# Modulation columns of four chunks by TensorE from the loaded weights, and x loaded first, in the head of a two-layer diffusion backbone

## The chip, the cores and the metric

The kernel runs on one core of one Trainium2 chip, as one program for both layers. The time is the device time of one execution in microseconds, taken as the median of several runs. The profile comes from one more execution, recorded by the hardware profiler. TensorE (PE in the profile, its weight loads PEld) multiplies matrices into PSUM, VectorE (DVE), ScalarE (ACT) and GpSimd (POOL) work element by element, and SyncE (SP) issues most of the transfers.

## The reference

Two layers work on 1024 latent tokens and 256 context tokens of width 1024. The head of the kernel computes the beginning of layer 0: shift and scale of the modulation, the normalised and modulated tokens, and the first quarter of the `v` half of `h @ w_in`.

```python
def rms_norm(x, g):
    xf = x.astype(jnp.float32)
    y = xf * lax.rsqrt(jnp.mean(xf * xf, axis=-1, keepdims=True) + EPS)
    return (y * g.astype(jnp.float32)).astype(x.dtype)

def modulate(h, shift, scale):
    return h * (1 + scale) + shift

def chunk_mlp(h, w_in, ln_g, ln_b, w_s, b_s, w_out):
    z = jax.nn.gelu(h @ w_in)
    u, v = jnp.split(z, 2, axis=-1)
    v = layer_norm(v, ln_g, ln_b)
    ...

    silu_c = jax.nn.silu(c)
    for i in range(DEPTH):
        mod_lat = (silu_c @ ada_w[i] + ada_b[i])[:, None, :]
        ...
        sh1, sc1, g1, sh2, sc2, g2 = jnp.split(mod_lat, 6, axis=-1)
        ...
        h = modulate(rms_norm(x, norm_g[i, 0]), sh1, sc1)
        ...
            y = chunk_mlp(h, a_w_in[j], a_ln_g[j], a_ln_b[j], a_w_s[j], a_b_s[j], a_w_out[j])
```

All is float32. The kernel splits each float32 operand of the large products into a high and a low part of type float32r and forms three products (high by high, high by low, low by high).

## The kernel before, in words

The ten token tiles of 128 rows are worked in two groups: five latent tiles (LAT), then three latent and two context tiles. The head (lines 580 to 780 of the kernel) is the part of the first group that the change touches. It works in eight chunks of 128 model columns (k = 0 to 7).

Names in the head:

- `xn0` holds the five token tiles, loaded by five transfers (lines 679 and 680) and normalised row by row: ACT squares and sums, GpSimd takes the power, DVE multiplies (lines 686 to 688).
- `flip_x(k)` transposes chunk k of the five tiles on TensorE (five transposes) into `pts[k]`, a PSUM tile of two banks. There are two such tiles, and one is taken by the head's sums, so `flip_x(k + 1)` waits until `x_hi(k)` has read `pts[k]`.
- `AdaBlock(k0, nk)` loads the columns of ada_w for shift and scale of `nk` chunks (two of 128 or 256 columns at a time), `accum` multiplies the eight row blocks by the conditioning vector and sums them on DVE, `total` sums over the partitions on TensorE with a vector of ones (`2 * nk` matmuls of one column), and `finish` adds bias and norm weight on DVE into the modulation columns. The buffers of the loaded columns have the tag `act`, six of them, 512 KB each.
- `x_hi(k)` applies scale and shift on ACT (two instructions) and casts the high part; `x_lo(k)` subtracts for the low part on DVE.
- `w_load(u)`, `w_hi(u)`, `w_lo(u)` load a block of 256 rows of w_in into one of three buffers `raw` and split it, on ACT and DVE; block u serves the chunks 2u and 2u + 1.
- `head_mm(k, part)` is one of three groups of five float32r matmuls with 512 columns, one per token tile, summed over all k in five banks.

The order of the work in the head is written by hand: `pins` holds the names of VectorE, ScalarE, TensorE and SyncE (line 584), and each of these engines then keeps the order of the program. A step that waits therefore holds up what stands behind it on its engine. Lines 676 to 778 are that order. Before, there are five blocks: b0 and b1 of one chunk, b2, b3 and b4 of two chunks each. Behind the head `pins` is cleared, and `gmlp` goes on with the same buffers `raw` for w_in and for the columns of the next modulations.

## Time and profile before

| | before |
|---|---|
| median of 3 runs | 2856.6 us (2850.05 to 2860.5) |
| profiled execution | 2860.88 us, span 2859.1 us |
| DVE SCALAR_TENSOR_TENSOR on the blocks' columns (`acc<-act`) | 35 in the head, 22.5 us |
| TensorE 128x1 matmuls in the head (`psA<-ones,acc`) | 32, 4.8 us |
| last matmul of the head starts | 65.07 us |
| mean granted clock | 0.988 |

In the page each engine has its busy time, its share of the span and its number of instructions. A row of a stretch gives the time and number of instructions of each engine in that stretch, then the clock granted to TensorE (1 is full), the share of the DMA engines and what they moved. A row of the timeline gives start, duration, engine, operation, tile written and tiles read, and in brackets the idle time ahead of it and what ended it. Nearly every instruction has line 50, that of a helper; the tile names tell them apart: `y` is `xn0`, `act` the loaded columns, `acc` the sums on DVE, `big` the high and low parts of x, `wh` and `wl` those of the weights.

### The profile page before, as it was taken

To read this page: it belongs to the slowest core of one execution; us is meant where nothing else is said; L and a number is where in the kernel's file an instruction comes from. 1 tells how busy PE (TensorE), PEld (TensorE's weight loads), DVE (VectorE), ACT (ScalarE), POOL (GpSimd) and SP (SyncE) were. 2 spreads that over 40 slices of the span, in tenths; PEclk is the share of its full clock that TensorE was granted. 3 is DMA by queue.
4 is the path that set the end of the run, shared out by engine and by line. 5 is a ranking of instruction groups with operands and counts; after the bars stand their busy time and mean duration, and the time that the engine had idled before them with its cause. 6 is when DMAs were issued, how large, how long until landed. Compare 5 with 4: busy or idle time off the path is not lost.

```text
span 2859.1 us, 40314 instructions
## 1 busy us (share of the span) xinstructions
PE 2741.8 (96%) x14570; PEld 2354.1 (82%) x14570; DVE 2221.8 (78%) x3466; ACT 1391.2 (49%) x2291; POOL 616.6 (22%) x806
## 2 busy tenths in 40 slices
PE   7999999999989999999999899999998999999998
PEld 5798887898889888888788778888887888888786
DVE  6567684787779899887776568898887788888776
ACT  4333242232367444455434545777876444445433
POOL 1164021360210212111000124543333121220000
PEclk9999999999999999999999999999999999999999
DMA  7775457554488355467855565347577345545753
GB/s 260 251 234 166 145 161 227 177 167 131 171 249 240 103 170 162 157 217 238 287 169 184 188 212 186 115 145 239 181 242 220 126 162 182 160 144 198 248 177 125
DMA packets 436335, 537.13 MB, mean 188 GB/s; under 512 B 20004, under 2 KB 300452, under 8 KB 436135
## 3 DMA queue, kind: packets, MB, share of 16 engines
q1 hardware_dynamic: 379575, 470.84, 51.4%
q10 hardware_dynamic: 55408, 59.52, 6.2%
q0 software_dynamic: 1152, 4.19, 0.4%
q8 instruction: 115, 1.88, 0.3%
q14 instruction: 85, 0.70, 0.1%
HBM read 414.40 MB, written 120.07 MB: 187 GB/s over the span
## 4 chain that ended last, share of the span: by engine, by line
PE 65%; DVE 13%; DMA 11%; ACT 5%; issue 4%; POOL 2%; SPq 1%; ACTq 0%; DVEq 0%; POOLq 0%
PE psB L50 48%; PE psA L50 16%; DVE row L50 3%; DVE wl L50 3%; DMA raw<-in_ada_w_dram 3%; DVE tmp L50 1%; DVE acc L50 1%; ACT wh L50 1%; ACT tmp L50 1%; DMA xT<-row 1%; DMA raw<-in_a_w_in_dram 1%; DVE y L50 1%; POOL sm L50 1%; DMA raw<-in_f_w_up_dram 1%; DMA raw<-in_f_w_down_dram 1%
## 5 line engine op out<-in xcount | busy, mean ns | idle before, releaser
L50 PE MATMUL psB<-cmb,wh 128*128 128x512 f32 (+2 forms) x2584 | 750.3, 374 | 7.2 <-ACT row L50 6.2
L50 PEld LDWEIGHTS psB<-cmb,wh 128*128 128x128 f32 x2584 | 471.9, 188 | 98.4 <-ACT row L50 8.1
L50 PE MATMUL psB<-cmb,wl 128*128 128x512 f32 (+2 forms) x1292 | 483.2, 374 | 0.2 <-DVE wl L50 0.2
L50 ACT CAST wh<-raw 128x1024 fp32r<-128x1024 f32 (+1 forms) x313 | 265.1, 863 | 441.6 <-PE psB L50 165.5
L50 DVE TENSOR_TENSOR wl<-raw,wh 128x1024 fp32r<-128x1024 f32 (+1 forms) x313 | 307.6, 997 | 106.6 <-ACT wh L50 104.9
L50 PEld LDWEIGHTS psB<-cmb,wl 128*128 128x128 f32 x1292 | 243.2, 188 | 44.0 <-DVE wl L50 0.8
L50 PE MATMUL psB<-wh,big 128*128 128x512 f32 x816 | 271.1, 398 | 3.7 <-ACT big L50 1.3
L50 ACT CAST wh<-row 128x1024 fp32r<-128x1024 f32 (+1 forms) x196 | 162.5, 834 | 186.8 <-DVE row L50 92.3
L50 PE MATMUL psB<-wh,act 128*128 128x512 f32 x640 | 200.1, 390 | 0.8 <-DVE tmp L50 0.8
L50 DVE TENSOR_TENSOR wl<-row,wh 128x1024 fp32r<-128x1024 f32 (+1 forms) x196 | 185.2, 948 | 12.2 <-ACT wh L50 11.8
L50 PE MATMUL psA<-big,wh 128*128 128x320 f32 x1024 | 193.2, 310 | 0.3 <-ACT row L50 0.3
L50 POOL TENSOR_TENSOR row<-raw,raw 128x512 f32<-128x512 f32 x44 | 68.5, 1558 | 574.2 <-DMA raw<-in_f_w_up_dram 490.8
L50 PEld LDWEIGHTS psB<-wh,big 128*128 128x128 f32 x816 | 154.3, 190 | 39.9 <-ACT tmp L50 2.4
L50 DVE SCALAR_TENSOR_TENSOR acc<-raw,ccols,acc 128x1024 f32<-128x1024 f32 x98 | 126.7, 1311 | 75.8 <-DMA raw<-in_ada_w_dram 75.5
L50 DVE SCALAR_TENSOR_TENSOR row<-row,cwcols,row 128x1024 f32<-128x1024 f32 (+2 forms) x142 | 152.6, 1075 | 39.2 <-ACT row L50 22.7
L50 ACT CAST ah<-raw 128x1024 fp32r<-128x1024 f32 x80 | 77.6, 974 | 201.6 <-PE psB L50 80.8
L50 DVE TENSOR_TENSOR row<-row,row 128x512 f32<-128x512 f32 (+4 forms) x169 | 155.9, 926 | 19.9 <-DMA row<-actd 12.2
L50 POOL TENSOR_SCALAR row<-row,sm,sm 128x128 f32<-128x128 f32 x160 | 144.1, 919 | 115.2 <-DMA row<-vscr 99.3
L50 PEld LDWEIGHTS psA<-big,wh 128*128 128x128 f32 x1024 | 159.9, 188 | 0.7 <-ACT row L50 0.5
L50 PE MATMUL psB<-wl,big 128*128 128x512 f32 x408 | 157.2, 395 | 0.9 <-DVE wl L50 0.9
L50 DVE TENSOR_TENSOR al<-raw,ah 128x1024 fp32r<-128x1024 f32 x80 | 90.2, 1128 | 71.9 <-ACT ah L50 71.6
L50 PE MATMUL psB<-row,wh 128*128 128x256 f32 x744 | 136.9, 286 | 8.2 <-ACT wh L50 6.7
(279 smaller groups left out, 6226.0 us busy)
## 6 DMA issues: line engine op xcount, KB each, us to landing
raw<-in_f_w_up_dram SPq DMA_DIRECT2D x121, 512.0 KB, 4.8
raw<-in_ada_w_dram SPq DMA_DIRECT2D x88, 512.0 KB, 4.4
raw<-in_a_w_in_dram SPq DMA_DIRECT2D x64, 512.0 KB, 4.8
wh<-woscr SPq DMA_DIRECT2D x48, 512.0 KB, 4.1
row<-actd SPq DMA_DIRECT2D x44, 512.0 KB, 5.5
actc<-row SPq DMA_DIRECT2D x44, 512.0 KB, 4.1
raw<-actc SPq DMA_DIRECT2D x40, 512.0 KB, 3.6
actd<-row SPq DMA_DIRECT2D x39, 512.0 KB, 2.7
```

Source lines behind the costliest of these rows:

```text
L50: ins = fn(*a, **kw)
```

## The change

A new class `AdaColumn` loads shift and scale columns of one chunk (two transfers of 512 KB) and forms the modulation columns on TensorE alone: for each of the two, eight matmuls with the loaded 128x128 block of ada_w as the stationary operand and one column of the conditioning vector as the moving one, summed in PSUM. Chunks 0 to 3 are made this way (b0 to b3); chunks 4 and 5 (b4) and 6 and 7 (b6) stay with `AdaBlock`. The rows of x are loaded ahead of the first columns. `w_hi(0)` is cast in two halves and comes after `x_hi(0)`. The order of the head is written anew.

```diff
+    def finish_block(block):
+        k0, nk = block.k0, block.nk
+        p = pts[k0][:, 1, 256:256 + 2 * nk]
+        for s in (1, 0):
+            finish_cols(0, s, 0, p[:, s * nk:(s + 1) * nk], slice(k0, k0 + nk))
+
...
+    class AdaColumn:
+        def __init__(self, k0):
+            self.k0, self.nk, self.rv = k0, 1, {}
             for s in (1, 0):
-                finish_cols(0, s, 0, p[:, s * nk:(s + 1) * nk], slice(k0, k0 + nk))
+                self.rv[s] = t_act((P, KD, P), F32)
+                Q.dma_start(self.rv[s], ada_w[0, :, s * D + k0 * P:s * D + (k0 + 1) * P]
+                            .rearrange("(k p) n -> p k n", p=P))
+
+        def total(self):
+            p = pts[self.k0][:, 1, 256:258]
+            for s in (1, 0):
+                for k in range(KD):
+                    T.matmul(p[:, s:s + 1], self.rv[s][:, k, :], ccols[:, k:k + 1], start=(k == 0), stop=(k == KD - 1))
+
+        def finish(self):
+            finish_block(self)
...
-        S.copy(hi, raws[nb, u])
+        for c in ((0, 512), (512, 1024)) if (nb, u) == (0, 0) else ((0, 1024),):
+            S.copy(hi[:, slice(*c)], raws[nb, u][:, slice(*c)])
...
-    b0 = AdaBlock(0, 1)
     adab, aR = load_rows([ada_b.rearrange("l (k p) -> (l k) p", p=P)])
     ngr, nR = load_rows([norm_g.rearrange("l i (k p) -> (l i k) p", p=P)])
     for i, t in enumerate(LAT):
         Q.dma_start(xn0[:, i, :], src_row(0, t))
+    b0 = AdaColumn(0)
     w_load(0)
-    b1 = AdaBlock(1, 1)
+    b1 = AdaColumn(1)
+    b2 = AdaColumn(2)
...
```

The new order, from the first transposes to where it joins the old one:

```python
    flip_x(0); b0.total(); b0.finish(); x_hi(0); w_hi(0); x_lo(0); w_lo(0)
    b3 = AdaColumn(3); w_load(1)
    head_mm(0, 0); flip_x(1); b1.total(); b1.finish(); x_hi(1)
    head_mm(0, 1); head_mm(0, 2); x_lo(1)
    b4 = AdaBlock(4, 2)
    flip_x(2); b2.total(); b2.finish(); x_hi(2); w_hi(1); b4.accum(range(0, 2))
    head_mm(1, 0); head_mm(1, 1); head_mm(1, 2); x_lo(2); w_lo(1)
    w_load(2); b6 = AdaBlock(6, 2)
    flip_x(3); b3.total(); b3.finish(); x_hi(3); b4.accum(range(2, 4))
    head_mm(2, 0); head_mm(2, 1); head_mm(2, 2); x_lo(3); b4.accum(range(4, 8)); w_hi(2)
    flip_x(4); head_mm(3, 0); head_mm(3, 1); b4.total(); b4.finish(); x_hi(4); w_lo(2)
    head_mm(3, 2); x_lo(4); b6.accum(range(0, 2)); w_load(3)
    flip_x(5); x_hi(5); x_lo(5); b6.accum(range(2, 5))
    head_mm(4, 0); head_mm(4, 1); head_mm(4, 2)
    flip_x(6); w_hi(3); b6.accum(range(5, 8))
    head_mm(5, 0); b6.total(); b6.finish(); x_hi(6); w_lo(3); x_lo(6)
    head_mm(5, 1); head_mm(5, 2); w_load(0, 1); flip_x(7)
```

From `flip_x(7)` on the order is as before.

## The prediction

> **What bounds the kernel now.** I read the page first, then the head by stretches, then the chain of waits, then single instructions of TensorE in order of time.

> ```profile
> span 2859.1 us, 40314 instructions
> ...
> PE 2741.8 (96%) x14570; PEld 2354.1 (82%) x14570; DVE 2221.8 (78%) x3466; ACT 1391.2 (49%) x2291; POOL 616.6 (22%) x806
> ```

> ```profile
> core 0: us, PE busy (x) PEld busy (x) DVE busy (x) ACT busy (x) POOL busy (x), PEclk, DMA share, GB/s
> 31.90:65.10 33.20, 31.64 (x160) 24.99 (x159) 25.52 (x42) 16.39 (x24) 0.00 (x0) 1.00 0.66 214
> ```

> The whole is TensorE's: 96% busy. The change touches only the head, from the start to the last head matmul. TensorE is busy for 31.64 of the 33.20 us between 31.90 and 65.10; DVE, which the change relieves, has 7.7 us to spare there. Before 31.90 it is otherwise:

> ```profile
> 6.36 8.23 DMA y<-in_x_dram
> ...
> 24.01 2.57 DMA act<-in_ada_w_dram
> ```

> The chain runs through the loading of x, then through DVE's sums that wait for columns of ada_w. So the head has two parts: up to about 32 us it waits for data, from there TensorE is the bound. Work taken from DVE helps the first part, work given to TensorE lengthens the second. The same in single instructions:

> ```profile
> 19.44 0.47 PE L50 MATMUL psA<-ident,y 128*128 128x128 f32 x1 [0.99 <-DVE y L50]
> 19.71 0.85 PE L50 MATMUL psA<-ones,acc 128*128 128x1 f32 x4
> ...
> 23.08 2.08 PE L50 MATMUL psB<-wh,big 128*128 128x512 f32 x4 [1.34 <-ACT big L50]
> ...
> 26.73 1.02 PE L50 MATMUL psA<-ones,acc 128*128 128x1 f32 x4 [1.15 <-DVE acc L50]
> 27.61 2.05 PE L50 MATMUL psB<-wh,big 128*128 128x512 f32 x4
> ...
> 29.89 1.91 PE L50 MATMUL psB<-wl,big 128*128 128x512 f32 x4
> ...
> 31.94 0.71 PE L50 MATMUL psA<-ident,y 128*128 128x128 f32 x5
> ...
> 35.12 1.05 PE L50 MATMUL psA<-ones,acc 128*128 128x1 f32 x8 [0.15 <-DVE acc L50]
> 36.04 1.17 PE L50 MATMUL psB<-wl,big 128*128 128x512 f32 x4
> ...
> 39.93 1.09 PE L50 MATMUL psB<-wh,big 128*128 128x512 f32 x4
> ...
> 41.08 1.07 PE L50 MATMUL psB<-wl,big 128*128 128x512 f32 x4
> ...
> 42.22 0.71 PE L50 MATMUL psA<-ident,y 128*128 128x128 f32 x5
> 42.69 1.18 PE L50 MATMUL psB<-wh,big 128*128 128x512 f32 x4
> ```

> Two prices can be read off. A head group of five 512-column matmuls takes 41.08 - 39.93 = 1.15 us late in the head, but 31.94 - 29.89 = 2.05 to 29.89 - 27.61 = 2.28 us early: up to 31.8 us TensorE runs at half clock, though the granted-clock column has no record there. And `b0.total()`, two matmuls in the source, is four in the trace: an F32 matmul is issued twice. Each 128x1 pair (weight load and matmul) takes (27.61 - 26.73)/4 = 0.22 us at half clock and (36.04 - 35.12)/8 = 0.115 at full.

> **The change part by part.** First, the columns 0 to 3. DVE loses the sums of b0, b1 and b2:

> ```profile
> L50 DVE SCALAR_TENSOR_TENSOR acc<-act,ccols,acc 128x512 f32<-128x512 f32 x21 | 15.7, 748 | 0.4
> ...
> L50 DVE SCALAR_TENSOR_TENSOR acc<-act,ccols,acc 128x256 f32<-128x256 f32 x14 | 6.8, 484 | 0.5
> ```

> About 6.8 us of the small ones and a third of the large (5.2) go, with their starts some 13 us of DVE, none of it on the path after 32 us. TensorE gets, per column, 2 streams x 8 chunks = 16 F32 matmuls = 32 pairs: 7.0 us at half clock, 3.7 at full. Removed are 4, 4 and 8 pairs.

> Second, x first. The issues that go from ahead of x, and x's own:

> ```profile
> 1.52 2.05 SPq L50 DMA_DIRECT2D act<-in_ada_w_dram  x4
> ...
> 4.79 3.15 SPq L50 DMA_DIRECT2D y<-in_x_dram  x5
> ```

> ```profile
> 15.86 1.06 ACT L50 ACTIVATE tmp<-y 128x1024 bf16<-128x1024 f32 x1
> ```

> ```profile
> 15.00:20.00 5.00, 1.98 (x6) 1.11 (x7) 2.26 (x3) 2.96 (x5) 3.08 (x6) 1.00 1.09 343
> ```

> x is issued 2.1 us earlier, and 1.05 MB no longer lie ahead of it, 3.0 us at 343 GB/s. If the rows of x only share the engines with what is issued behind them, it is nothing; I take 2.5, near the 2.1 of the issue: the last transpose of chunk 0 ends at 17.4 instead of 19.9. b0's 1.05 MB now land 3 us behind the last row of x, which was squared at 15.86 and now at 13.4 or so: 16.4, just in time.

> Third, the way to the first matmul. `b0.total()` runs with nothing before it but transposes, at half clock: 17.4 + 32 x 0.22 = 24.4. From the end of that step (19.71 + 0.85) to the first head matmul it was 23.08 - 20.56 = 2.5 us (finish, modulation, cast). `w_hi(0)`, which ran before, now follows `x_hi(0)` on ACT, and its first half is waited for:

> ```profile
> 17.15 1.04 ACT L50 CAST wh<-raw 128x1024 fp32r<-128x1024 f32 x1
> ```

> Half of 1.04 is 0.5, so the first head matmul starts at 24.4 + 3.0 = 27.4 instead of 23.08.

> Fourth, from there to the end of the head, first all at full clock: 24 groups x 1.15 = 27.6; 7 transposing steps x 0.5 (42.69 - 42.22) = 3.5; b1 to b3, 96 x 0.115 = 11.0; b4 and b6 8 pairs each, 1.8. Waits: one of the 0.5 us kind remains (chunk 5 behind a block's chunk 4), and one is new.

> ```profile
> PE psA L50 <- ACT tmp L50: 1.4, 3, 0.5
> ```

> ```profile
> 45.08 0.95 PE L50 MATMUL psA<-ones,acc 128*128 128x1 f32 x8
> ```

> ```profile
> L50 DVE TENSOR_SCALAR acc<-act,ccols 128x512 f32<-128x512 f32 x3 | 1.4, 481 | 0.0
> ```

> ```profile
> 48.49 0.82 DVE L50 TENSOR_TENSOR big<-tmp,big 128x640 fp32r<-128x640 f32 x1 [0.56 <-ACT big L50]
> ```

> The new one: all eight sums of b6 stand behind `x_lo(4)` on DVE, and b6's total is one group earlier than its like was. The like of `x_lo(4)` ended at 49.31, 3.3 us after the block total of 45.08 that feeds it (ended 46.03); then come 0.48 + 7 x 0.75 = 5.7 us of sums and 0.82 of `x_lo(5)`: 9.8 us, while TensorE has five groups, two transposing steps and a wait, 7.2. It waits 2.6. Sum: 27.6 + 3.5 + 11.0 + 1.8 + 0.5 + 2.6 = 47.0, head end 74.4. It now ends here, with the last matmul's successor at 65.30:

> ```profile
> 65.07 0.39 PE L50 MATMUL psA<-wl,big 128*128 128x512 f32 x1
> 65.30 0.39 PE L50 MATMUL psA<-wh,big 128*128 128x512 f32 x1
> ```

> That is +9.1 with the clock left at full after the first column. But the clock does not stay:

> ```profile
> 35.24:38.66 3.42, 2.96 (x18) 2.17 (x18) 2.05 (x7) 1.86 (x3) 0.00 (x0) 1.00 0.88 291
> ...
> 96.68:100.10 3.42, 0.00 (x0) 0.00 (x0) 2.30 (x4) 0.00 (x0) 0.00 (x0) 1.00 0.89 320
> 100.10:103.51 3.41, 2.99 (x7) 2.41 (x8) 0.81 (x3) 0.00 (x0) 0.00 (x0) 0.50 0.44 142
> ...
> 127.40:130.82 3.42, 3.29 (x23) 2.93 (x23) 1.86 (x3) 1.42 (x3) 2.81 (x4) 1.00 0.44 136
> 130.82:134.23 3.41, 3.41 (x14) 2.91 (x13) 1.92 (x3) 0.38 (x2) 0.00 (x0) 0.50 1.07 326
> ```

> ```profile
> 127.67 1.95 PE L50 MATMUL psB<-ones,acc 128*128 128x1 f32 x16
> 129.48 0.48 PE L50 MATMUL psB<-wl,big 128*128 128x512 f32 x1
> ```

> The clock changes on a grid of 3.41 us. An idle stretch (96.68) is followed by one at 0.50, and that, with 2.99 us of wide matmuls in it, by full clock again. The stretch at 127.40 is what matters: TensorE was busy for 3.29 of 3.42 us, 1.8 of them with 16 one-column pairs and 1.3 (39%) with wide matmuls, and the next stretch is at 0.50 all the same. So such pairs count for next to nothing. At 35.24 five wide matmuls (1.15 us, 34%), five transposes and 8 pairs kept the clock: the border lies near 35 to 40% of wide work. In the changed kernel a column and its transposing step make 3.7 + 0.5 = 4.2 us without wide work, longer than a stretch; two stretches hold at most 6.8 - 4.2 = 2.6 us of it, so one of them falls below the border unless they split it evenly. [...]

> The price: from 27.4 on, `mm(0,0)`, b1 and `mm(0,1)`, `mm(0,2)` are at half clock, since no stretch full of wide work comes before the last two: 3 x 1.0 + 32 x 0.105 + 0.6 (two transposing steps, 0.3 each by estimate) = 7.0. Then b2 and b3 each bring one or two stretches at half, 1.7 to 3.4 us; I take 2.6 each. Together 12.2, head end 86.6, +21.3. With a lucky phase of the grid (up during `mm(0,1)`, one stretch per column or none) about 12; unlucky 23.

> Edits at nothing: eight issues of 512 KB replace 16 of 256 KB on SP. b3's buffers are b0's, so on SP `w_load(1)` and b4 stand behind b0's total (24.4); they are wanted after 45 us. b4's last buffers wait for b2's total, about 47, wanted near 60. If either came late, TensorE would wait for it one to one. DVE's b4 sums stand ahead of `x_lo(2)` and `w_lo(1)`, and their data wait for b1's total (37) and land about 42, ahead of b2's finish.

> Does the delay last to the end? The loads after the head go through three buffers, freed by `w_lo(3)` and `w_lo(0, 1)`, both of which stand behind head steps. I find nothing behind the head that starts by itself, so I carry the delay whole. The profiled execution took 2860.88 us, 1.8 beyond its span, and would come to 2882.2; it is 4.3 over the median of 2856.6. On the median the sum is 2877.9, taken as 2878, 0.7% slower.

> **The rivals.** (1) The pairs do count as work, and the clock stays. Then b0 lifts it itself after one stretch: 3.4 + 16.5 x 0.115 = 5.3 us, first head matmul at 25.7, head end at 25.7 + 47.0 = 72.7, +7.4: 2864, no measurable change. For it speaks the stretch at 35.24, against it that at 127.40.

> (2) Not slower: the pairs go nearly free, because weight loads slip in beside other work, and the head is freed of DVE's sums and of ada_w ahead of x. With a price p per pair the head ends at 17.4 + 32p + 3.0 + 36.0 + 96p = 56.4 + 128p. It decides at p = 0.07 us: below, the change gains, at most 8.9 us: 2848. The rows show 0.113 (16 pairs in 1.81 us) with wide matmuls on both sides. Even so it would hardly pass 0.5%.

> (3) The order of DVE or SP stalls TensorE more than I see (b4 or b6 late): +25 to +30, 2882 to 2887.

> **How the numbers follow.** The forecast 0.62, rival 1 0.24, rival 2 0.08, rival 3 0.06. About 0.5% (14.3 us) is what a measurement of this kernel can tell from no change. Slower by more: the forecast except its lucky end (0.57), rival 3 (0.06), a little of rival 1: 0.64. Faster by more: 0.04, a part of rival 2 with the 10 us by which runs differ. The rest is 0.32. The range runs from rival 1 less 4 us, 2860, to the unlucky phase and the scatter above it, 2884.

> **What would show it.** Right: 32 pairs per column in TensorE's timeline, 0.2 us each in column 0; first head matmul near 27, last near 85; granted clock of 0.5 behind columns 2 and 3; a wait of 2 to 3 us for DVE before b6's total; transposes of chunk 0 done near 17. Wrong: the granted clock at 1.00 from 30 us on (rival 1), pairs under 0.07 us (rival 2), a head that is late but a span that is not.

## The result and the profile after

| | before | after |
|---|---|---|
| median of 6 runs each | 2851.07 us (2846.16 to 2860.5) | 2875.44 us (2864.74 to 2879.28) |
| ratio | | 1.0078, 95% interval 1.0054 to 1.0102 |
| span of the profiled execution | 2859.1 us | 2872.3 us |
| last matmul of the head starts | 65.07 us | 83.92 us |

By the medians the change makes the kernel slower by 24 us (15 to 29 by the interval of the ratio); 2878 was forecast. The page of the changed kernel, its span and first row:

```profile
span 2872.3 us, 40499 instructions
...
PE 2757.4 (96%) x14682; PEld 2371.0 (83%) x14682; DVE 2208.6 (77%) x3445; ACT 1390.5 (48%) x2292; POOL 620.3 (22%) x806
```

TensorE has 112 more matmuls: 4 columns of 32 pairs are 128, and 16 went. It is 15.6 us busier. DVE is 13.2 us less busy, near the 13 us that were counted. The single instructions of TensorE in the head, in order of time:

```profile
16.39 0.48 PE L50 MATMUL psA<-ident,y 128*128 128x128 f32 x1 [0.99 <-DVE y L50]
16.66 6.83 PE L50 MATMUL psA<-ccols,act 128*128 128x1 f32 x32
26.52 2.08 PE L50 MATMUL psB<-wh,big 128*128 128x512 f32 x4 [3.03 <-ACT wh L50]
...
29.88 6.83 PE L50 MATMUL psA<-ccols,act 128*128 128x1 f32 x32
36.57 2.05 PE L50 MATMUL psB<-wh,big 128*128 128x512 f32 x4
...
38.85 1.91 PE L50 MATMUL psB<-wl,big 128*128 128x512 f32 x4
...
41.95 3.82 PE L50 MATMUL psA<-ccols,act 128*128 128x1 f32 x32
45.63 2.05 PE L50 MATMUL psB<-wh,big 128*128 128x512 f32 x4
...
51.11 3.63 PE L50 MATMUL psA<-ccols,act 128*128 128x1 f32 x32
54.60 1.32 PE L50 MATMUL psB<-wh,big 128*128 128x512 f32 x4
...
73.47 1.05 PE L50 MATMUL psA<-ones,acc 128*128 128x1 f32 x8 [2.02 <-DVE acc L50]
...
83.92 0.39 PE L50 MATMUL psA<-wl,big 128*128 128x512 f32 x1
```

The four columns are the four rows with x32: 6.8 us at half clock for columns 0 and 1, 3.8 and 3.6 at full for 2 and 3. A wide matmul is one of 512 columns, and a head group has five of them. The group at 36.57 takes 2.05 us for its first four, as does the one at 45.63, behind column 2: half clock. The row at 73.47 is the foreseen wait for DVE's eight sums of b6. In the traces before and after, the granted clock is recorded as 1.00 or 0.50 and nothing else, and each of the 22 records of a trace starts a whole number of 3.413 us behind the first one. Stretches of this grid, with the granted clock behind the POOL column:

```profile
38.41:41.83 3.42, 3.42 (x11) 2.72 (x10) 0.83 (x1) 0.72 (x1) 0.00 (x0) 1.00 0.38 126
41.83:45.24 3.41, 3.41 (x33) 3.41 (x32) 0.00 (x0) 0.00 (x0) 0.00 (x0) 1.00 0.08 19
45.24:48.65 3.41, 3.41 (x11) 2.83 (x11) 1.95 (x6) 2.31 (x4) 0.00 (x0) 0.50 0.88 286
48.65:52.07 3.42, 3.42 (x24) 2.98 (x23) 1.63 (x2) 0.50 (x1) 0.00 (x0) 1.00 0.45 156
52.07:55.48 3.41, 3.41 (x28) 3.27 (x29) 0.67 (x4) 0.19 (x1) 0.00 (x0) 1.00 0.40 120
55.48:58.90 3.42, 3.42 (x10) 2.64 (x9) 2.78 (x5) 2.62 (x4) 0.00 (x0) 0.50 0.84 271
```

In every row TensorE is busy throughout, and yet the clock falls to 0.50 behind the two stretches that hold columns 2 and 3. (At 38.41 the column shows 1.00 for want of a record, the first being at 41.83, as it is at 31.83 in the kernel before; the wide group of 38.85, 1.91 us for its first four, tells that it is half.) DVE meanwhile idles: 0.00 at 41.83.

### The profile page after: what moved, and what is told of

Its sections match the earlier page's. It is cut to its first block, busy times and chain, and to the rows that moved or that the text cites. A ratio compares the mean times of both kernels' runs of the same rounds, so it can differ in the third digit from the quotient of the medians.

```text
span 2872.3 us, 40499 instructions
## 1 busy us (share of the span) xinstructions
PE 2757.4 (96%) x14682; PEld 2371.0 (83%) x14682; DVE 2208.6 (77%) x3445; ACT 1390.5 (48%) x2292; POOL 620.3 (22%) x806
## 4 chain that ended last, share of the span: by engine, by line
PE 63%; DVE 13%; DMA 11%; issue 5%; ACT 4%; POOL 2%; SPq 0%; ACTq 0%; DVEq 0%; POOLq 0%
PE psB L50 46%; PE psA L50 17%; DVE row L50 4%; DMA raw<-in_ada_w_dram 4%; DVE wl L50 3%; DVE acc L50 1%; DMA raw<-in_a_w_in_dram 1%; ACT wh L50 1%; DVE tmp L50 1%; DMA xT<-row 1%; DMA raw<-in_f_w_up_dram 1%; ACT tmp L50 1%; POOL sm L50 1%; DVE y L50 1%; ACT row L50 1%
## 5 line engine op out<-in xcount | busy, mean ns | idle before, releaser
L50 PE MATMUL psB<-cmb,wh 128*128 128x512 f32 (+2 forms) x2584 | 749.3, 374 | 9.7 <-ACT row L50 7.5
L50 PEld LDWEIGHTS psB<-cmb,wh 128*128 128x128 f32 x2584 | 471.0, 188 | 101.3 <-ACT row L50 10.2
L50 PE MATMUL psB<-cmb,wl 128*128 128x512 f32 (+2 forms) x1292 | 482.5, 373 | 0.1
L50 ACT CAST wh<-raw 128x1024 fp32r<-128x1024 f32 (+1 forms) x314 | 265.3, 861 | 430.6 <-PE psB L50 171.4
L50 DVE TENSOR_TENSOR wl<-raw,wh 128x1024 fp32r<-128x1024 f32 (+1 forms) x313 | 307.8, 998 | 108.1 <-ACT wh L50 107.0
L50 PEld LDWEIGHTS psB<-cmb,wl 128*128 128x128 f32 x1292 | 242.9, 188 | 43.8 <-DVE wl L50 0.5
L50 PE MATMUL psB<-wh,big 128*128 128x512 f32 x816 | 273.0, 401 | 5.9 <-ACT wh L50 3.7
L50 ACT CAST wh<-row 128x1024 fp32r<-128x1024 f32 (+1 forms) x196 | 162.6, 835 | 188.9 <-DVE row L50 97.6
L50 PE MATMUL psB<-wh,act 128*128 128x512 f32 x640 | 200.1, 391 | 0.8 <-DVE tmp L50 0.8
L50 POOL TENSOR_TENSOR row<-raw,raw 128x512 f32<-128x512 f32 x44 | 70.6, 1604 | 571.5 <-DMA raw<-in_f_w_up_dram 467.9
L50 PE MATMUL psA<-big,wh 128*128 128x320 f32 x1024 | 193.2, 310 | 0.3 <-ACT row L50 0.3
L50 DVE TENSOR_TENSOR wl<-row,wh 128x1024 fp32r<-128x1024 f32 (+1 forms) x196 | 185.4, 949 | 9.9 <-ACT wh L50 9.7
L50 PEld LDWEIGHTS psB<-wh,big 128*128 128x128 f32 x816 | 155.6, 192 | 41.5 <-ACT wh L50 4.2
L50 DVE SCALAR_TENSOR_TENSOR row<-row,cwcols,row 128x1024 f32<-128x1024 f32 (+2 forms) x142 | 151.9, 1070 | 39.6 <-ACT row L50 22.8
L50 DVE SCALAR_TENSOR_TENSOR acc<-raw,ccols,acc 128x1024 f32<-128x1024 f32 x98 | 126.4, 1308 | 71.7 <-DMA raw<-in_ada_w_dram 71.6
L50 ACT CAST ah<-raw 128x1024 fp32r<-128x1024 f32 x80 | 77.8, 975 | 201.9 <-PE psB L50 80.8
L50 DVE TENSOR_TENSOR row<-row,row 128x512 f32<-128x512 f32 (+4 forms) x169 | 156.0, 927 | 20.5 <-DMA row<-actd 11.5
L50 POOL TENSOR_SCALAR row<-row,sm,sm 128x128 f32<-128x128 f32 x160 | 145.8, 926 | 112.8 <-DMA row<-vscr 96.6
L50 PEld LDWEIGHTS psA<-big,wh 128*128 128x128 f32 x1024 | 159.9, 188 | 0.7 <-ACT row L50 0.5
L50 PE MATMUL psB<-wl,big 128*128 128x512 f32 x408 | 157.8, 397 | 0.3 <-DVE wl L50 0.3
L50 DVE TENSOR_TENSOR al<-raw,ah 128x1024 fp32r<-128x1024 f32 x80 | 90.3, 1128 | 73.7 <-ACT ah L50 73.5
L50 PE MATMUL psB<-row,wh 128*128 128x256 f32 x744 | 135.3, 284 | 8.2 <-ACT wh L50 6.5
```

The lines of the kernel that those rows point to most:

```text
L50: ins = fn(*a, **kw)
```

## The experiments

Three theories stood against each other: the pairs cost their time and also let the clock fall (the forecast); the pairs cost their time alone; the new order, with x first, costs the time by itself. All head ends below are the start of the last head matmul, 65.07 before and 83.92 after. Five of the runs (burst, spread, half the pairs, two columns, column 3 spread) were executed once, at 2863, 2857, 2857, 2863 and 2879 us; executions of one kernel lie more than 10 us apart, so their whole times decide little, and the head ends and the granted clock are compared instead.

**A burst and a spread.** In the kernel before, 32 unused F32 matmuls of one column (64 pairs), either in two bursts or divided among wide groups.

```diff
+    def pairs_at(k, n):
+        for _ in range(n):
+            T.matmul(pts[k][:, 1, 300:301], ident, ones[:, 0:1], start=True, stop=True)
...
     flip_x(5)
+    pairs_at(5, 16)
...
     flip_x(7)
+    pairs_at(7, 16)
```

> The kernel before with work added: 16 F32 matmuls of one column (32 pairs, result unused) in one burst after the transposes of chunk 5, and 16 more after those of chunk 7. Theory (the pairs cost 0.115 us each and count as no work for the clock): each burst takes 3.7 us, and with the 0.5 us of transposes it leaves a stretch of the 3.41 us grid without wide work, so a granted clock of 0.50 follows behind at least one of the two bursts, 1.7 us more each time; last head matmul 65.1 + 7.4 + 1.7 to 3.4 = 74.2 to 75.9. Rival (the pairs are work like any other): clock 1.00 from 32 us to 75 us, last head matmul 72.5.

```diff
     head_mm(4, 0)
+    pairs_at(5, 5)
     head_mm(4, 1)
+    pairs_at(5, 5)
     head_mm(4, 2)
+    pairs_at(5, 6)
...
     head_mm(6, 0)
+    pairs_at(7, 5)
...
     head_mm(6, 1)
+    pairs_at(7, 5)
     head_mm(6, 2)
+    pairs_at(7, 6)
```

> The kernel before with the same 32 unused F32 matmuls of one column (64 pairs) added, but five, five and six of them behind the three groups of chunk 4 and of chunk 6, so that wide work fills some 45% of every stretch. Theory: only the pairs' own time is paid, the clock stays at 1.00, last head matmul at 65.1 + 64 x 0.115 = 72.5. Rival (the clock falls by the sum of pairs, not by their closeness): as the burst, 74 to 76. A third view (weight loads slip in beside wide matmuls): well under 72, towards 65.

The burst, stretches of the grid and the instructions in them:

```profile
48.60:52.02 3.42, 2.96 (x26) 2.56 (x24) 2.78 (x5) 1.53 (x3) 0.00 (x0) 1.00 1.00 324
52.02:55.43 3.41, 3.41 (x16) 3.41 (x17) 0.45 (x1) 0.29 (x1) 0.00 (x0) 0.50 0.04 14
55.43:58.85 3.42, 3.42 (x9) 2.65 (x9) 1.76 (x3) 2.50 (x4) 0.00 (x0) 0.50 0.00 0
...
69.09:72.50 3.41, 3.41 (x13) 3.02 (x13) 0.00 (x0) 1.64 (x3) 0.00 (x0) 0.50 0.50 154
72.50:75.92 3.42, 3.42 (x10) 2.65 (x9) 3.06 (x3) 3.40 (x5) 0.00 (x0) 0.50 0.02 4
```

```profile
50.06 5.04 PE L50 MATMUL psA<-ones,ident 128*128 128x1 f32 x32
...
66.41 4.38 PE L50 MATMUL psA<-ones,ident 128*128 128x1 f32 x32
```

The spread, the stretch from the last change of the clock to the end of its head, then ten pairs and the wide group behind them:

```profile
38.60:42.02 3.42, 3.42 (x12) 2.75 (x10) 2.95 (x4) 2.98 (x5) 0.00 (x0) 0.50 0.65 199
42.02:72.74 30.72, 29.73 (x176) 24.91 (x176) 18.82 (x30) 12.80 (x18) 0.00 (x0) 1.00 0.52 169
```

```profile
51.53 1.24 PE L50 MATMUL psA<-ones,ident 128*128 128x1 f32 x10
...
53.87 1.17 PE L50 MATMUL psA<-ones,ident 128*128 128x1 f32 x10
```

The burst's head ends at 79.83, the spread's at 74.37, with the same instructions. Both are 1.7 us late ahead of the added pairs already: the transposes of chunk 4 start at 43.91 and 43.96, before at 42.22. Most of that is a stretch at half near 38 to 42 us (the spread's row at 38.60; in the burst the group at 39.13 takes 2.06 us for its first four). Without it the spread adds 74.37 - 65.07 - 1.7 = 7.6 us, the pairs' own 7.4. Its bare 74.37 would fit the rival (74 to 76) as well; what decides is that no stretch at 0.50 follows its pairs. The burst adds 13.1 us: 7.4 for the pairs, and 5.7 more in four stretches at half, which can cost 4 x 1.7 = 6.8 at most. Here the theory (74.2 to 75.9) has the direction right and the size too small: two stretches fell behind each burst, not one. That the pairs are work like any other is refuted, and so is that weight loads slip in for nothing: ten pairs among wide groups take 1.17 to 1.24 us.

**Half the pairs** in the changed kernel; every other row block is left out of the sums, and so of the result:

```diff
-                for k in range(KD):
-                    T.matmul(p[:, s:s + 1], self.rv[s][:, k, :], ccols[:, k:k + 1], start=(k == 0), stop=(k == KD - 1))
+                for k in range(0, KD, 2):
+                    T.matmul(p[:, s:s + 1], self.rv[s][:, k, :], ccols[:, k:k + 1], start=(k == 0), stop=(k == KD - 2))
```

> The changed kernel with every other of the eight row blocks left out of the sums of columns 0 to 3 (the modulation is then of half the weights): 16 pairs per column instead of 32. Theory: 3.5 us less in b0 and in b1 (half clock), 1.8 less in b2 and b3, 10.6 in all, and the gap without wide work shrinks to 2.3 us, shorter than a stretch, so that one or both stretches at 0.50 behind b2 and b3 go too (1.7 each): last head matmul at 84.1 - 10.6 = 73.5 down to 70. Rival (the new order, its waits on SP and DVE, costs the time, not the pairs): little less than 84, at least 80.

```profile
35.50:71.00 35.50, 33.01 (x177) 27.22 (x178) 24.23 (x42) 17.98 (x26) 0.00 (x0) 1.00 0.65 210
```

The head ends at 70.67, 13.2 us earlier, and no stretch falls to 0.50 once the clock is up at 35.5. The pairs themselves are 10.3 of the 13.2 (3.4 each in columns 0 and 1, 1.7 and 1.8 in 2 and 3); the rest, 2.9, fits the two stretches at half that are gone, since TensorE's waits are those of the changed kernel (3.0, 2.0 and 0.5 us). The order, unchanged here, does not hold the head at 80 or later, as the rival had it.

**Two columns in the old order.** Only b0 and b1 by TensorE, x still behind b0:

```diff
...
-    b0 = AdaBlock(0, 1)
+    b0 = AdaColumn(0)
...
-    b1 = AdaBlock(1, 1)
+    b1 = AdaColumn(1)
...
-    b0.accum(range(KD))
...
-    b1.accum(range(0, 4))
...
-    b1.accum(range(4, 8))
```

> The old order, x behind the first columns, old blocks for chunks 2 to 7; only b0 and b1 are summed by TensorE, 32 pairs each, and their DVE sums are gone. Theory: 28 pairs more for b0 and 28 more for b1, both at half clock, 2 x 6.1 = 12.2 us, and the clock goes up later, one or two stretches (1.7 to 3.4); DVE's relief saves at most the waits of 1.2 us: last head matmul 65.1 + 11 to 16 = 76 to 81. Rival (the new order is at fault): at most 68, since the waits of TensorE for DVE's sums are gone.

The rows on TensorE, and DVE's first normalisation:

```profile
17.87 6.83 PE L50 MATMUL psA<-ccols,act 128*128 128x1 f32 x32
...
29.51 6.82 PE L50 MATMUL psA<-ccols,act 128*128 128x1 f32 x32
```

```profile
10.91 0.75 DVE L50 TENSOR_SCALAR y<-y,rstT 128x1024 f32<-128x1024 f32 x1 [2.85 <-POOL rstT L50]
```

The same normalisation in the kernel before:

```profile
12.76 0.75 DVE L50 TENSOR_SCALAR y<-y,rstT 128x1024 f32<-128x1024 f32 x1
```

The head ends at 73.70, +8.6: between the two expectations, and less than mine. The 56 pairs more cost the 12 us (56 x 0.213), but two things were miscounted. The groups `head_mm(0, 0)` to `(0, 2)` ran at half clock before as well, up to 31.83 (2.08, 2.05 and 1.91 us for their first four, against 1.09 at 39.93), so the later rise of the clock (41.24 instead of 31.83) is no cost beside the columns' own. And DVE, free of b0's sums, starts on the rows of x at 10.91, not at 12.76 as before: the last transpose of chunk 0 ends at 18.1, 1.8 us earlier, though x was loaded no earlier. The wait of 1.2 us for DVE's sums of b1 goes too, which leaves 9 of the 12, near the 8.6.

**DVE's sums in the new order:**

```diff
-    b0 = AdaColumn(0)
+    b0 = AdaBlock(0, 1)
...
     flip_x(0)
+    b0.accum(range(KD))
     b0.total()
     b0.finish()
+    b1.accum(range(KD))
```

and likewise for b1, b2 and b3, whose sums stand one column ahead.

> The changed kernel with x first and its order, but columns 0 to 3 loaded as blocks of one chunk and summed by DVE (eight steps of 0.48 us each, placed one column ahead), TensorE only taking the two totals of each. Theory (the pairs and the clock are the whole loss): the head ends about where it did before, last matmul at 64 to 68, and the time is that of the kernel before within 0.3%. Rival (x first and the new order cost time of their own, through SP's and DVE's waits): last matmul at 75 or later, time 10 us or more above before.

```profile
PE psA L50 <- DVE y L50: 8.9, 5, 4.7
PE psA L50 <- DVE acc L50: 8.2, 4, 3.4
```

The ratio is 1.0023 (1.0012 to 1.0035), the head ends at 68.76. So of the 18.8 us that the head has grown, 15.1 go with TensorE's sums, and 3.7 stay when DVE does the sums in the new order: TensorE then waits 8.2 us for them, and the clock falls twice here too: the groups at 34.05 and 47.51 take 1.85 and 1.84 us for their first four, those ahead of them 1.17 and 1.08. That is a little over the 64 to 68 that I expected, and far from the rival; the interval of the time leaves out 1, so the new order with DVE's sums is not quite free.

**Column 3 spread in the changed kernel.** Its 32 pairs stand between the groups of chunk 1, and end up in the tile of chunk 2:

```diff
...
+    b3.home = 2
     head_mm(1, 0)
+    b3.some(range(0, 5))
     head_mm(1, 1)
+    b3.some(range(5, 10))
     head_mm(1, 2)
+    b3.some(range(10, 16))
...
+    b3.finish()
     flip_x(3)
-    b3.total()
-    b3.finish()
```

> The changed kernel with column 3's 32 pairs taken out of their burst and put between and behind the three groups of chunk 1, ten, ten and twelve pairs. Theory with a border for each direction (down under some 36% of wide work, up only over some 75%): column 2's burst still puts the clock to 0.50 near 45 us, and the mixed stretch behind it, 45% wide, cannot lift it, so chunk 1 and the pairs run at half clock, 13.3 us in place of some 9, and the last head matmul moves from 83.9 to 86 to 90. Rival (only bursts matter, and spreading them cures the clock): one stretch at 0.50 less than in the changed kernel, last head matmul near 82.

```profile
37.22:40.64 3.42, 3.42 (x31) 3.27 (x31) 0.00 (x0) 0.00 (x0) 0.00 (x0) 1.00 0.02 5
...
40.64:61.12 20.48, 19.88 (x71) 17.59 (x71) 6.86 (x14) 5.59 (x8) 0.00 (x0) 0.50 0.50 156
```

The head ends at 88.42, later than without the spreading. Column 2's burst puts the clock down at 40.64, and it stays down for six stretches. Five wide matmuls and ten pairs, the mix at which the clock stayed at 1.00 in the spread run, did not raise the fallen one here. In this execution the clock came up earlier, at 30.4 in place of 41.83 (the 32 pairs of column 1, from 29.74 on, take 3.95 us in place of 6.83), so that column 2 began at 38.07 in place of 41.95, and a stretch at half more fell behind the wait for b6 (the group at 78.80 takes 1.91 us for its first four, its like in the changed kernel 1.07): the 4.5 us between the two heads are not the spreading's price alone.

**Column 0 in TensorE's idle time.** The old order; the columns of chunk 0, loaded ahead of x, are summed before the transposes:

```diff
...
-    b0 = AdaBlock(0, 1)
+    b0 = AdaColumn(0)
...
-    b0.accum(range(KD))
+    pts[0] = psA()
+    b0.total()
...
     flip_x(0)
-    b0.total()
     w_hi(0)
```

> The kernel before, old order, with only column 0 summed by TensorE, and that before the transposes of chunk 0, while TensorE waits for x. Theory (what counts is whether the 32 pairs lie in idle time): 7.0 us at half clock from about 9 to 16, all before x is ready; DVE is free of 3.9 us of sums ahead of the rows of x, so the last transpose of chunk 0 ends near 18.1 instead of 19.9, the first head matmul starts near 20.6 instead of 23.08, and the last near 62.4 to 63.6 instead of 65.07; time 1.5 to 2.7 us less, below what a measurement can tell. Rival 1 (32 pairs cost TensorE wherever they are): last head matmul at 68 or later. Rival 2 (the loads of b2 set the pace): the first head matmul is earlier, the last is not.

```profile
8.07 6.99 PE L50 MATMUL psA<-ccols,act 128*128 128x1 f32 x32
...
20.28 2.08 PE L50 MATMUL psB<-wh,big 128*128 128x512 f32 x4 [1.44 <-ACT big L50]
```

The ratio to the kernel before is 0.9986 (0.9978 to 0.9994): this version is 2 to 6 us faster than the kernel before, and so the fastest of those that were run often enough to tell. Its 32 pairs at half clock cost nothing: they end at 14.9, and the last row of x is only ready for its transpose at 17.30 (19.44 before). The first head matmul starts 2.8 us earlier, the last at 62.25, also 2.8. The 1.5 to 2.7 us that I forecast for the time lie at the lower end of the interval.

## Why the prediction was right

Step by step, with what was measured. The last transpose of chunk 0 ends at 16.87 (17.4 forecast), column 0 at 23.5 (24.4), the first head matmul at 26.52 (27.4): these steps held. But the reason given for the first one was half wrong. Of the 3.0 us, the run with two columns shows that 1.8 come from DVE being free of b0's sums; x first is left with 1.2, where I gave it all 2.5. (x itself came 4.3 us earlier, its last row squared at 11.56 instead of 15.86; the rows then follow each other at 1.47 us, with DVE waiting for GpSimd's power, 0.72 us each.) I had put DVE's relief off the path, which holds after 32 us and not before.

The price of the pairs, 0.22 and 0.115 us, held in all four columns (0.21 twice, 0.115 and 0.109). The clock rose behind `mm(0,1)` and `mm(0,2)`, at 41.83, and fell behind columns 2 and 3, as forecast. I took one and a half stretches (2.6 us) for each of these, and it was one each, about 1.6 us. The wait for b6's sums was 2.0, not 2.6. With the 0.9 us of the first matmul these make some 3.5 us too much; the other terms were together 1 us too small, and the head end of 86.6 came out 2.5 us too late against 84.14.

Rival 1 is refuted by burst and spread, rival 2 by the pairs' time in every run. Rival 3 did not come about in the head: from the first head matmul on, the only other wait of TensorE is one of 0.5 us for ACT, which was forecast.

The step that the delay is carried whole held in its sum, not in its reason. I found nothing behind the head that goes by its own time; the waits of TensorE from 65 to 200 us before, and from 84 to 220 us after, say otherwise:

```profile
PE psA L50 <- DVE cwcols L50: 4.6, 1, 4.6
...
PE psA L50 <- ACT row L50: 0.3, 1, 0.3
```

```profile
PE psB L50 <- ACT tmp L50: 4.6, 1, 4.6
...
PE psA L50 <- DVE cwcols L50: 0.9, 1, 0.9
```

Of the delay of 18.8 us, 3.7 vanish in a wait that was there before (4.6 to 0.9). Then another of 4.6 us appears, and behind it three stretches at half clock:

```profile
144.23:154.47 10.24, 8.64 (x33) 7.76 (x33) 4.48 (x6) 2.74 (x6) 4.03 (x4) 0.50 0.64 190
```

The matmul that starts at 200 us before starts 20.7 us later after, and at 1170 us it is still 18.8. The second wait goes with the new order rather than with the length of the delay: it is 3.3 us with half the pairs, in the new order, where the head is only 5.6 us late, and of the runs of the old one it is 2.0 in the spread, 9.3 us late, and absent in the burst, 14.8 us late, and with two columns, 8.6 us late. Which step of the order sets it off was not tried and stays open. The two spans differ by 13.2 us alone: behind 250 us, where the delay is 20.5, the clock records of the profiled execution before add up to 59 us at half clock, those after to 45, and half of that difference is the 7 us by which the delay shrinks.

That the time itself was hit within 3 us is in part luck. The base of the forecast, a median of three runs, was 5.5 us above that of six; the head was forecast 2.5 us too late; and the time grew by 24.4 us by the medians, 5.5 more than the head, of which the delay of 20.7 at 200 us accounts for 1.9. The rest lies within the interval of 15 to 29.

## What to carry to other kernels

Before moving a sum from DVE to TensorE, ask which of the two is late at that place: the same 32 pairs cost nothing ahead of the transposes, where TensorE waited for x, and 3.6 to 6.8 us per column where it was the bound. Price it in issued instructions (here 16 F32 matmuls were 32 pairs of 0.115 us at full clock and 0.21 at half), and don't take TensorE's busy time for what keeps its clock up: here it was busy for all 3.41 us of the stretch at 41.83, which column 2 took up, and the next one was at 0.50. If such matmuls must be there, try them spread while the clock is still up: 64 pairs in two bursts brought four stretches at half, the same 64 among wide groups none.

## What the hardware showed that was not expected

Measured by the share of time, the border for falling and the one for rising differ. In the spread kernel a cycle of five wide matmuls (1.15 us) and ten pairs (53.87 - 51.53 = 2.34 us in all, 49% wide) kept a full clock. In the changed kernel with column 3 spread, five wide ones (2.28 us at half clock) and ten pairs made 46.67 - 42.40 = 4.27 us, 53% wide, and did not raise a fallen one:

```profile
42.40 2.05 PE L50 MATMUL psB<-wh,big 128*128 128x512 f32 x4
...
46.67 2.05 PE L50 MATMUL psB<-wh,big 128*128 128x512 f32 x4
```

The transposes are part of that work: counted single, stretches with up to 5.6 are followed by half and others with as little as 2.9 by full clock. The prediction did not see this when it read the border off the stretch at 35.24. In the kernel before, that stretch holds five wide matmuls and all five transposes (they start at 37.91, and it ends at 38.66), and the clock stays up. In the burst and the spread kernel, which are the same up to there, the transposes start at 38.24 and 38.28 and the stretch ends at 38.37 and 38.60, so that some of them fall outside; in both the next stretch is at half (0.50 in the spread's row at 38.60, 2.06 us for four wide matmuls in the burst). A shift of 0.3 us of the instructions against the grid decides there over a stretch at half clock.
